# Sliding-window scores as three fp32r products instead of plain fp32, in other banks, with two pieces of other work behind the first quad

## The chip, the cores and the metric

The kernel runs on one core of a Trainium2 chip. The metric is device time in microseconds (us) of one execution. The kernel before the change takes 2162.4 us (median of three runs, 2161.97 to 2162.98).

## What is computed

One step of a one-layer streaming encoder over a prompt of 1024 tokens and a sample of 64, 1024 features wide: retention and sliding-window attention side by side, then cross-attention to 256 memory tokens, then SwiGLU. The change touches the sliding-window attention (SWA): 16 query heads of 64 features share 2 heads of keys and values; a chunk of 64 tokens attends to itself and to the two chunks before it, 192 keys at most.

```python
CHUNK = 64
SWA_HEADS, SWA_KV_HEADS, SWA_HD = 16, 2, 64     # 8 query heads share one head of keys
def swa_attend(q, k, v, bias, sinks, valid):
    s = jnp.einsum('bnqhgd,bnkhd->bnhgqk', q, k, preferred_element_type=jnp.float32) * (SWA_HD ** -0.5)
    s = s + bias.astype(jnp.float32)
    ...
    m = jnp.maximum(jnp.max(s, axis=-1, keepdims=True), sink)
    e = jnp.exp(s - m)
    p = e / (jnp.sum(e, axis=-1, keepdims=True) + jnp.exp(sink - m))
    return jnp.einsum('bnhgqk,bnkhd->bnqhgd', p.astype(v.dtype), v)
```

## The kernel before, in words

All activations lie transposed, features on partitions and tokens on columns. Dense products don't run in plain fp32. `split` (L123 to 125) makes two operands of a tile: ACT copies it, rounded, to the type fp32r (`hi`, L124), and DVE subtracts that from the tile (`lo`, L125). `mm3` (L155 to 159) then adds up three fp32r products, hi x hi, hi x lo and lo x hi, on lines 157, 158 and 159. The large projections do the same in blocks of 128 x 272 columns (L223, L224, L226; recombined in L274), and their last step empties a bank of PSUM in L613 (DVE), scales in L619 (DVE), applies the activation in L621 (ACT) and stores from POOL's queue (L731).

The **SWA phase** (`swa_phase`, about 790 to 955 us of the profiled execution) comes right behind the last of these projections. It has two kinds of work, which are interleaved by hand on PE. The first is attention: 17 chunks of 64 queries (`c`, 0 to 16), in two halves each (`hf`); a chunk and a half are called a *quad* here, since it has four score matrices (two heads of keys `v`, two pairs of heads `i`, each 128 rows by up to 192 keys). The second is *filler*: the dense product of the retention's output with `w_ret_out`, in pieces of half a product, and ahead of it the four pieces (two products, 24 matmuls each) that make the last head's values of the memory.

The loop in `swa` runs i from -2 to 33. In each round PE gets, in this order: `weigh` of quad i-1 (probabilities times values, for a whole chunk), `scores` of quad i+2, `turn` of quad i (transposes of the probabilities), and as many pieces as the generator `fill` hands out. `in_order` makes each of these wait for the last matmul of the one before, so this order is PE's; the order on the other engines comes from a scheduler that keeps the named dependencies.

- `scores`: four plain fp32 matmuls a quad on L1004, the weights being 64 rows of a query tile, the moving operand 64 rows of `kT` with 64 (chunk 0), 128 (chunk 1) or 192 columns. The trace shows each as two instructions, so a quad has eight. Both heads `v` lie on different halves of the rows. The result is the PSUM tile `pss` (tag "s", two banks, one buffer).
- DVE reads each matrix with a fused bias-add and minimum (L1014, four a quad), then L1018. ACT takes four exponentials (L1020) and one for the sinks (L1022). DVE adds and inverts (L1023, L1024), POOL multiplies (L1026, L1031).
- `turn`: values' transposes (L981, copied by ACT on L983), probabilities' transposes (L1043, L1054; copied by ACT on L1047 and DVE on L1056). `weigh`: L1067 into `pout`, copied by DVE on L1071.
- filler: the last products' evacuation is L1229 for `ret` and L1200 for the memory values. Its PSUM tiles `pd` have two buffers, which the values' transposes share.

PSUM pools take banks in the order in which they are opened, so the tag "s" gets the first two, which the last block of the projections before has used. SBUF comes from eight slots per ring ("swin0" to "swin7"), cut by hand: `kT` (keys, 1216 columns), two query tiles of four chunks each, the bias, buffers `lds` for the filler, `vT` and its transposed blocks. Queries come in five loads of four chunks, issued by SP. `begin_swa` issues the phase's first loads while the last projections run; `first_low` (L1153) makes ten `lo` operands of the filler behind the first quad's reads, `later_operands` the others at fixed steps.

Of the kernel before, what the change touches and what calls it, by code (L numbers as in the profile page):

```python
# [11 lines left out]
F32 = mybir.dt.float32  # L12
F32R = mybir.dt.float32r
# [6 lines left out]
P = 128  # L20
# [89 lines left out]
class Kernel:  # L110
# [811 lines left out]
    def swa_phase(self):  # L922
        with ExitStack() as ctx:
            filler = []

            def fill():


                pieces = self.filler()
                yield []  # L930
                yield [pieces] * 6
                count, steps, done = 48 - 10, 2 * 17, 0
                for i in range(steps):
                    goal = count * (i + 1) // steps
                    yield [pieces] * (goal - done)
                    done = goal
                yield [pieces] * 8

            self.store_by = self.nc.gpsimd
            self.swa(ctx, fill())  # L940
            self.store_by = self.nc.sync
# [17 lines left out]
    def swa(self, ctx, fill):  # L959
        nc, tc, io = self.nc, self.tc, self.io  # L960
        if True:
            sw = self.sw = ctx.enter_context(tc.tile_pool(name="sw", bufs=5, reuse_waits="tile"))
            pw = ctx.enter_context(tc.tile_pool(name="pw", bufs=1, reuse_waits="tile", space=PSUM))
            mm = nc.tensor.matmul

            flat, kT, bias, qTs, sinks = self.flat, self.kT, self.bias, self.qTs, self.sinks
            vT = flat[5][:, :KC]
            vts = [flat[4][:, i * P:(i + 1) * P] for i in range(17)] + [flat[0][:, KC + i * P:KC + (i + 1) * P] for i in range(3)]

            def keep():  # L970
                for src, o in ((kT, "o_sk"), (vT, "o_sv")):
                    self.store(io[o][0], src[:, SEQ - P:SEQ])
                    self.store(io[o][1], src[:, SEQ + SMP:KC])

            vtok = {}

# [18 lines left out]

            def scores(c, hf):
                ks, j0, nk = keys(c)
                if hf == 0 and c % 4 == 0 and 0 < c < 13:
                    self.load_queries(qTs, c + 4)
                qT = qTs[c // 4 % 2]  # L1000
                pss = pw.tile([P, 2, 512], F32, tag="s", name="pss")
                for i in range(2):
                    for v in range(2):
                        self.last_mm = mm(pss[:, v, i * NKEY:i * NKEY + nk], qT[rows[v], 2 * hf + i, c % 4, :],  # L1004
                                          kT[rows[v], ks:ks + nk], start=True, stop=True).ins
                quad = lambda x: x.rearrange("p (v h i) -> p v h i", v=2, h=2)[:, :, hf, :]
                snk = quad(sinks)
                t = sw.tile([P, 2, 2, NKEY], F32, tag="t", name="t")
                ps = pss[:, :, :2 * NKEY].rearrange("p v (i n) -> p v i n", n=NKEY)
                bs = bias.rearrange("p (v h i) n -> p v h i n", v=2, h=2)  # L1010
                nm = sw.tile([P, 2, 2], F32, tag="nm", name="nm")
                for v, i in units:
                    u = quad(self.minus)[:, v, i:i + 1]
                    nc.vector.tensor_tensor_reduce(t[:, v, i, :nk], ps[:, v, i, :nk], bs[:, v, hf, i, j0:], -0.125, u,  # L1014
                                                   ALU.add, ALU.min, nm[:, v, i:i + 1])
                den = sw.tile([P, 2, 2], F32, tag="den", name="den")
                es = sw.tile([P, 2, 2], F32, tag="es", name="es")
                ready = nc.vector.tensor_tensor(out=es, in0=snk, in1=nm, op=ALU.add).ins  # L1018
                for v, i in units:
                    nc.scalar.activation(t[:, v, i, :nk], t[:, v, i, :nk], AF.Exp, bias=nm[:, v, i:i + 1], scale=-1.0,  # L1020
                                         accum_out=den[:, v, i:i + 1])
                self.marks.append((ready, nc.scalar.activation(es, es, AF.Exp).ins))  # L1022
                nc.vector.tensor_tensor(out=den, in0=den, in1=es, op=ALU.add)  # L1023
                nc.vector.reciprocal(den, den)  # L1024
                p, n, e = t.rearrange("p v i n -> p (v i) n")[:, :, :min(nk, P)], min(nk, P), None
                nc.gpsimd.tensor_tensor(out=p, in0=p, op=ALU.mult,  # L1026
                                        in1=den.rearrange("p v i -> p (v i)").unsqueeze(2).broadcast_to([P, 4, n]))
                if nk == NKEY:
                    e = sw.tile([P, 2, 2, 64], F32, tag="e", bufs=4, name="e")
                    for v in range(2):  # L1030
                        nc.gpsimd.tensor_tensor(out=e[:, :, v ^ hf, :], in0=t[:, v, :, P:], op=ALU.mult,  # L1031
                                                in1=den[:, v, :].unsqueeze(2).broadcast_to([P, 2, 64]))
                live[c, hf] = t, e

            def turn(c, hf):
                ks, j0, nk = keys(c)
# [23 lines left out]
            def weigh(c, hf):  # L1060
                if hf == 0:
                    return
                parts = live.pop((c, "parts"))
                po = pw.tile([P, 2, 512], F32, tag="out", name="pout")
                for j, part in enumerate(parts):
                    for h, v, val, pT in part:
                        self.last_mm = mm(po[rows[v], h, :256], val[:, rows[v]], pT, start=j == 0, stop=j == len(parts) - 1).ins  # L1067
# [13 lines left out]
            for i in range(-2, n):  # L1081
# [8 lines left out]
                if i == -2:  # L1090
                    with tc.high_priority(), tc.issue_after(self.last_operand):
                        self.tokens(vT, 1, "cvT")
                if i == 2:
                    with tc.issue_after(self.last_operand):
                        self.load_queries(qTs, 4)
                if i == 8:
                    with tc.issue_after(self.last_operand):
                        keep()
# [3 lines left out]

    def begin_swa(self):

        tc, flat = self.tc, [t.rearrange("p a b -> p (a b)") for t in self.ring_tiles(0, KT, "swin", F32)]
        self.flat, self.kT = flat, flat[0][:, :KC]
        self.bias = flat[2][:, :NPAIR * NKEY].rearrange("p (a b) -> p a b", b=NKEY)
        self.qTs = [t[:, :16 * 2 * 64].rearrange("p (i c e) -> p i c e", i=4, c=4) for t in (flat[1], flat[7])]
        self.lds = [t[:, i * 384:(i + 1) * 384] for t in (flat[3], flat[6]) for i in range(5)]
        with tc.high_priority():  # L1110
            self.tokens(self.kT, 0, "ckT")
            self.load_queries(self.qTs, 0)
            for e in range(2):
                src = self.d_rb.rearrange("(p e) c -> e c p", e=2)[e, 63:63 + 64 * 255, :]
                src = src.rearrange("(i c) p -> i p c", c=255)[:, :, :NKEY]
                self.loaded = self.load(self.bias[e * 64:(e + 1) * 64], src)
        self.rets = [self.rings[1].tile(f"ret{k}", slot=i) for k, i in enumerate((0, 1, 4, 5, 6, 7, 2, 3))]
        self.marks = []
        self.first_loads()

    def tokens(self, dst, i, cache):
        self.load(dst[:, :SEQ], self.d_skv[i, :, :SEQ])
# [39 lines left out]
                    self.last_operand = self.load(x, self.d_gate[0][k, :, c0:c0 + n])  # L1162
                self.split(x, self.rets[k][:, 0, c0:c0 + n], self.rets[k][:, 1, c0:c0 + n])

    def load_queries(self, qTs, c):
        nq = min(4, 17 - c)
        src = self.d_sq[:, :, c:c + nq].rearrange("i p c a q -> p i (c a q)")
        self.load(qTs[c // 4 % 2][:, :, :nq, :].rearrange("p i c e -> p i (c e)"), src)

    def ring_tiles(self, i, n, what, dt=F32R):  # L1170
        return [self.rings[i].tile(f"{what}{k}", dt) for k in range(n)]
# [719 lines left out]
```

## Time and profile before

| what | value |
|---|---|
| median of three runs | 2162.4 us (2161.97 to 2162.98) |
| profiled execution, device time | 2165.55 us |
| its span | 2163.7 us |
| mean granted clock of PE | 0.996 |
| plain score matmuls (L1004), instructions | 272, from 790.6 to 951.7 us |

The profile names engines PE (matmul), PEld (its weight loads), DVE, ACT, POOL and SP. A row of a timeline gives start, duration, engine, line, operation, output <- input, tile and element type, and in brackets the idle time of the engine ahead of it with what ended it. Rows on consecutive instructions of one kind are joined (x8). A row of groups gives the count, the sum in us, the mean in ns, and the idle time ahead. fp32r operands are printed as f32 on PE.

### The profile page before, as it was taken

What the parts mean: (1) busy time and instruction counts of PE and PEld (TensorE: products, weight loads), DVE (VectorE), ACT (ScalarE), POOL (GpSimd) and SP (SyncE); (2) the same over time, 40 slices, a digit from 0 to 9 for tenths busy, and PEclk for the clock granted to TensorE, in tenths of its full rate; (3) what the DMA queues carried; (4) which work ended last, traced back from release to release, by engine and by line L of the source; (5) the groups of instructions that cost most, each with busy time, mean ns of one, the idle gap of its engine ahead of it and who ended that gap; (6) DMA issues with size and microseconds to landing.
All of it is one profiled execution on the core that took longest, in us unless ns stands there. A gap on an engine that the chain in (4) does not pass through costs nothing. (4 is left out here: it accounts for less than half of the span.)

```text
span 2163.7 us, 41722 instructions
## 1 busy us (share of the span) xinstructions
PE 2136.0 (99%) x16371; PEld 2084.6 (96%) x16371; DVE 1551.7 (72%) x2912; ACT 874.0 (40%) x1894; POOL 532.4 (25%) x448
## 2 busy tenths in 40 slices
PE   9999999999999999999999999999999999999997
PEld 9999999999999997789999999999999999999997
DVE  8987979786677568656545555678777777777597
ACT  8343434344444356553233333343223222344243
POOL 0000000022353125540000000015556555523531
PEclk9999999999999999999999999999999999999999
DMA  7334454435345485336442121412342232384333
GB/s 263 123 126 123 131 149 129 129 113 159 111 141 190 158 263 173 117 112 211 145 135 92 40 69 61 153 61 101 120 154 88 99 126 92 124 305 153 112 116 112
DMA packets 169893, 290.85 MB, mean 134 GB/s; under 512 B 39266, under 2 KB 96546, under 8 KB 169698
## 3 DMA queue, kind: packets, MB, share of 16 engines
q1 hardware_dynamic: 161666, 269.02, 38.7%
q0 software_dynamic: 3424, 10.82, 1.4%
q10 hardware_dynamic: 4608, 8.36, 1.0%
q8 instruction: 129, 2.11, 0.4%
q14 instruction: 66, 0.54, 0.1%
HBM read 196.97 MB, written 91.16 MB: 133 GB/s over the span
## 5 line engine op out<-in xcount | busy, mean ns | idle before, releaser
L124 ACT CAST wq<-raw 128x512 fp32r<-128x512 f32 (+1 forms) x499 | 302.1, 614 | 564.9 <-PE pq L226 228.8
L125 DVE TENSOR_TENSOR wq<-raw,wq 128x512 fp32r<-128x512 f32 (+1 forms) x499 | 426.8, 860 | 139.0 <-ACT wq L124 136.0
L223 PE MATMUL pq<-T,wq 128*128 128x272 f32 x1832 | 490.6, 287 | 1.7 <-ACT wq L124 0.6
L224 PE MATMUL pq<-T,wq 128*128 128x272 f32 x1832 | 492.0, 288 | 0.0
L224 PE MATMUL pq<-B,wq 128*128 128x272 f32 x1592 | 427.1, 288 | 1.0 <-DVE B L125 1.0
L223 PE MATMUL pq<-B,wq 128*128 128x272 f32 x1592 | 425.4, 287 | 0.1
L226 PE MATMUL pq<-T,wq 128*128 128x272 f32 x1832 | 382.7, 289 | 1.9 <-DVE wq L125 1.9
L201 POOL TENSOR_TENSOR raw<-raw 128x512 f32<-128x512 f32 (+1 forms) x44 | 64.0, 1454 | 1259.0 <-DVE wq L125 531.4
L223 PEld LDWEIGHTS pq<-T,wq 128*128 128x128 f32 x1832 | 344.3, 188 | 3.7 <-issue 1.2
L224 PEld LDWEIGHTS pq<-T,wq 128*128 128x128 f32 x1832 | 343.9, 188 | 0.8 <-issue 0.7
L226 PE MATMUL pq<-B,wq 128*128 128x272 f32 x1592 | 332.0, 289 | 0.0
L224 PEld LDWEIGHTS pq<-B,wq 128*128 128x128 f32 x1592 | 298.8, 188 | 2.4 <-DVE B L125 1.9
L223 PEld LDWEIGHTS pq<-B,wq 128*128 128x128 f32 x1592 | 298.9, 188 | 0.3 <-ACT stage L621 0.3
L226 PEld LDWEIGHTS pq<-T,wq 128*128 128x128 f32 x1832 | 289.6, 189 | 3.6 <-DVE wq L125 2.4
L226 PEld LDWEIGHTS pq<-B,wq 128*128 128x128 f32 x1592 | 251.7, 189 | 0.9 <-issue 0.7
L274 DVE TENSOR_TENSOR u<-pq,u 128x544 f32<-128x544 f32 x177 | 127.1, 719 | 78.5 <-PE pq L226 78.1
L613 DVE TENSOR_TENSOR stage<-pq,u 128x544 f32<-128x544 f32 x112 | 80.1, 717 | 31.0 <-PE pq L226 25.1
L157 PE MATMUL pd<-xc,wq 128*128 128x256 f32 (+1 forms) x256 | 74.5, 291 | 0.0
L159 PE MATMUL pd<-xc,wq 128*128 128x256 f32 (+1 forms) x256 | 74.1, 289 | 0.0
L158 PE MATMUL pd<-xc,wq 128*128 128x256 f32 (+1 forms) x256 | 73.7, 288 | 0.0
L1539 POOL TENSOR_TENSOR stage<-stage,rstd_f 128x544 f32<-128x544 f32 x40 | 63.9, 1606 | 39.1 <-ACT stage L1538 39.1
L204 POOL TENSOR_TENSOR raw<-raw 128x512 f32<-128x512 f32 (+1 forms) x44 | 58.9, 1338 | 52.6 <-DVE wq L125 50.1
(388 smaller groups left out, 4515.3 us busy)
## 6 DMA issues: line engine op xcount, KB each, us to landing
hl<-d_op SPq DMA_DIRECT2D x85, 272.0 KB, 5.3
d_qkv<-stage SPq DMA_DIRECT2D x44, 272.0 KB, 2.3
d_op<-stage SPq DMA_DIRECT2D x44, 272.0 KB, 2.2
d_op<-ht SPq DMA_DIRECT2D x44, 272.0 KB, 3.4
raw<-w_gate SPq DMA_DIRECT2D x22, 512.0 KB, 3.6
raw<-w_up SPq DMA_DIRECT2D x22, 512.0 KB, 5.0
raw<-w_down SPq DMA_DIRECT2D x16, 512.0 KB, 4.9
d_gate<-stage ACTq DMA_DIRECT2D x28, 272.0 KB, 2.9
```

Source lines behind the costliest of these rows:

```text
L124: self.last_cast = self.nc.scalar.copy(hi, src).ins
L125: return self.nc.vector.tensor_tensor(out=lo, in0=src, in1=hi.bitcast(F32), op=ALU.subtract).ins
L157: mm(ps, wh, xh, start=start, stop=False)
L158: mm(ps, wh, xl, start=False, stop=False)
L159: self.last_mm = mm(ps, wl, xh, start=False, stop=stop).ins
L201: tt(out=a11, in0=a11, in1=a21, op=sub)
L223: mm(ps[:, c, :HC], w[:, 0, ks], x[:, 0, cs], start=start, stop=False)
L224: mm(ps[:, c, :HC], w[:, 0, ks], x[:, 1, cs], start=False, stop=False)
L226: self.last_mm = mm(ps[:, c, :HC], w[:, 1, ks], x[:, 0, c * HC:(c + 1) * HC], start=False, stop=stop).ins
L274: add = lambda out, a, b: nc.vector.tensor_tensor(out=out, in0=a, in1=b, op=ALU.add)
L613: nc.vector.tensor_tensor(out=o, in0=ps, in1=sb, op=ALU.add)
L1539: nc.gpsimd.tensor_tensor(out=g, in0=g, in1=r[t], op=ALU.mult)
```

## The change

1. `scores` forms each matrix as three fp32r products, q hi x k hi, q hi x k lo and q lo x k hi. A quad has 12 instructions on PE in place of eight.
2. The keys are split once, 256 columns and then 960, in `begin_swa`. Each half of a chunk's queries (128x256) is split by `split_queries`, the first two in `begin_swa`, the others at the end of `scores`, two halves ahead.
3. Queries are loaded chunk by chunk, 17 loads, into six raw buffers.
4. `pout` gets a pool of its own, opened first, so it takes the two banks that tag "s" had, and "s" the two behind them.
5. `fill` hands out two of the memory values' four pieces between the first and the second quad, and four behind the second, where it handed out none and six.
6. Other slots: `vT` takes over the keys' raw buffer, the bias lies in slot 1 and is loaded earlier, the outputs of the keys (`o_sk`) are stored in `begin_swa`, and `lds` and `vts` are cut anew.

On PE, at the start of the phase, the order changes as follows (`swin_9666` and `swin_9667` are the raw keys and queries, `swin_9668` the `hi` parts, `swin_9669` the `lo` parts of both, `ms` the memory, x2 the two heads `v`):

```order
 L226 MATMUL pq<-T_626,wq 128x272 x2
-L1004 MATMUL pss<-swin_9666,swin_9667 128x64 x8
+L1002 MATMUL pss<-swin_9668 128x64 x2
+L1002 MATMUL pss<-swin_9669,swin_9668 128x64 x2
+L1002 MATMUL pss<-swin_9668,swin_9669 128x64 x2
+L1002 MATMUL pss<-swin_9668 128x64 x2
+L1002 MATMUL pss<-swin_9669,swin_9668 128x64 x2
+L1002 MATMUL pss<-swin_9668,swin_9669 128x64 x2
 L157 MATMUL pd<-wq,ms_7429 128x256
```

The two first quads, which stood together, now stand apart: the second comes 24 products of the values later. On DVE the split of the keys and of the first queries comes in among the last projection's recombinations:

```order
 L274 TENSOR_TENSOR u_9454<-pq,u_9452 128x544
+L125 TENSOR_TENSOR swin_9669<-swin_9666,swin_9668 128x256
+L125 TENSOR_TENSOR swin_9669<-swin_9667,swin_9668 128x256
+L125 TENSOR_TENSOR swin_9669<-swin_9666,swin_9668 128x960
+L125 TENSOR_TENSOR swin_9669<-swin_9667,swin_9668 128x256
 L125 TENSOR_TENSOR wq<-mw,wq 128x512
```

Four subtractions were added there, ahead of a weight's. Behind the first quad's reads DVE has, after the change (`swin_9670` is a buffer of raw queries in the rows of L125 and of the filler in L1222, the memory values' evacuation):

```order
+L1168 TENSOR_TENSOR ret_9686<-swin_9672,ret_9686 128x384
+L1168 TENSOR_TENSOR ret_9687<-swin_9670,ret_9687 128x384
+L1021 TENSOR_TENSOR den<-den,es 128x4
+L125 TENSOR_TENSOR swin_9669<-swin_9670,swin_9668 128x256
+L1222 TENSOR_SCALAR swin_9670<-pd,mtok 128x256
+L125 TENSOR_TENSOR swin_9669<-swin_9670,swin_9668 128x256
+L1012 ISA t,nm<-pss,swin_9667,minus 128x64
```

The evacuation moved ahead of the second quad's reads, with a query's subtraction on either side of it. The diff:

```diff
--- before.py
+++ after.py
@@ -927,8 +927,8 @@
 
 
                 pieces = self.filler()
-                yield []
-                yield [pieces] * 6
+                yield [pieces] * 2
+                yield [pieces] * 4
                 count, steps, done = 48 - 10, 2 * 17, 0
                 for i in range(steps):
                     goal = count * (i + 1) // steps
@@ -960,17 +960,16 @@
         nc, tc, io = self.nc, self.tc, self.io
         if True:
             sw = self.sw = ctx.enter_context(tc.tile_pool(name="sw", bufs=5, reuse_waits="tile"))
+            pout = ctx.enter_context(tc.tile_pool(name="po", bufs=1, reuse_waits="tile", space=PSUM))
             pw = ctx.enter_context(tc.tile_pool(name="pw", bufs=1, reuse_waits="tile", space=PSUM))
             mm = nc.tensor.matmul
 
-            flat, kT, bias, qTs, sinks = self.flat, self.kT, self.bias, self.qTs, self.sinks
-            vT = flat[5][:, :KC]
-            vts = [flat[4][:, i * P:(i + 1) * P] for i in range(17)] + [flat[0][:, KC + i * P:KC + (i + 1) * P] for i in range(3)]
+            flat, bias, sinks = self.flat, self.bias, self.sinks
+            vT = self.kT
+            vts = [flat[s][:, a + i * P:a + (i + 1) * P] for s, a, n in ((5, 0, 17), (4, 1664, 4)) for i in range(n)]
 
             def keep():
-                for src, o in ((kT, "o_sk"), (vT, "o_sv")):
-                    self.store(io[o][0], src[:, SEQ - P:SEQ])
-                    self.store(io[o][1], src[:, SEQ + SMP:KC])
+                self.keep("o_sv")
 
             vtok = {}
 
@@ -995,14 +994,13 @@
 
             def scores(c, hf):
                 ks, j0, nk = keys(c)
-                if hf == 0 and c % 4 == 0 and 0 < c < 13:
-                    self.load_queries(qTs, c + 4)
-                qT = qTs[c // 4 % 2]
                 pss = pw.tile([P, 2, 512], F32, tag="s", name="pss")
+                q, k = [x[(2 * c + hf) % 3] for x in self.qhl], [x[:, ks:ks + nk] for x in self.khl]
                 for i in range(2):
-                    for v in range(2):
-                        self.last_mm = mm(pss[:, v, i * NKEY:i * NKEY + nk], qT[rows[v], 2 * hf + i, c % 4, :],
-                                          kT[rows[v], ks:ks + nk], start=True, stop=True).ins
+                    for a, b in ((0, 0), (0, 1), (1, 0)):
+                        for v in range(2):
+                            self.last_mm = mm(pss[:, v, i * NKEY:i * NKEY + nk], q[a][rows[v], i, :], k[b][rows[v], :],
+                                              start=a + b == 0, stop=a == 1).ins
                 quad = lambda x: x.rearrange("p (v h i) -> p v h i", v=2, h=2)[:, :, hf, :]
                 snk = quad(sinks)
                 t = sw.tile([P, 2, 2, NKEY], F32, tag="t", name="t")
@@ -1031,6 +1029,7 @@
                         nc.gpsimd.tensor_tensor(out=e[:, :, v ^ hf, :], in0=t[:, v, :, P:], op=ALU.mult,
                                                 in1=den[:, v, :].unsqueeze(2).broadcast_to([P, 2, 64]))
                 live[c, hf] = t, e
+                self.split_queries(2 * c + hf + 2)
 
             def turn(c, hf):
                 ks, j0, nk = keys(c)
@@ -1061,7 +1060,7 @@
                 if hf == 0:
                     return
                 parts = live.pop((c, "parts"))
-                po = pw.tile([P, 2, 512], F32, tag="out", name="pout")
+                po = pout.tile([P, 2, 512], F32, tag="out", name="pout")
                 for j, part in enumerate(parts):
                     for h, v, val, pT in part:
                         self.last_mm = mm(po[rows[v], h, :256], val[:, rows[v]], pT, start=j == 0, stop=j == len(parts) - 1).ins
@@ -1090,9 +1089,10 @@
                 if i == -2:
                     with tc.high_priority(), tc.issue_after(self.last_operand):
                         self.tokens(vT, 1, "cvT")
-                if i == 2:
+                if i == -1:
                     with tc.issue_after(self.last_operand):
-                        self.load_queries(qTs, 4)
+                        for c in range(2, 6):
+                            self.load_queries(c)
                 if i == 8:
                     with tc.issue_after(self.last_operand):
                         keep()
@@ -1102,21 +1102,36 @@
 
     def begin_swa(self):
 
-        tc, flat = self.tc, [t.rearrange("p a b -> p (a b)") for t in self.ring_tiles(0, KT, "swin", F32)]
+        tc = self.tc
+        flat = [self.rings[0].tile(f"swin{i}", F32R if i in (2, 3) else F32).rearrange("p a b -> p (a b)") for i in range(KT)]
+        part = lambda *rows: [flat[s][:, a + i * w:a + (i + 1) * w] for s, a, n, w in rows for i in range(n)]
         self.flat, self.kT = flat, flat[0][:, :KC]
-        self.bias = flat[2][:, :NPAIR * NKEY].rearrange("p (a b) -> p a b", b=NKEY)
-        self.qTs = [t[:, :16 * 2 * 64].rearrange("p (i c e) -> p i c e", i=4, c=4) for t in (flat[1], flat[7])]
-        self.lds = [t[:, i * 384:(i + 1) * 384] for t in (flat[3], flat[6]) for i in range(5)]
+        self.khl = [flat[i][:, :KC] for i in (2, 3)]
+        self.qhl = [[t.rearrange("p (i e) -> p i e", i=2) for t in part((i, KC, 3, 256))] for i in (2, 3)]
+        self.qraw = [t.rearrange("p (i e) -> p i e", i=4) for t in part((1, 1536, 1, 512), (4, 0, 1, 512), (7, 0, 4, 512))]
+        self.lds = part((0, KC, 2, 384), (6, 0, 5, 384), (4, 512, 3, 384))
+        self.bias = flat[1][:, :NPAIR * NKEY].rearrange("p (a b) -> p a b", b=NKEY)
+        self.split_done = []
         with tc.high_priority():
             self.tokens(self.kT, 0, "ckT")
-            self.load_queries(self.qTs, 0)
+            self.load_queries(0)
             for e in range(2):
                 src = self.d_rb.rearrange("(p e) c -> e c p", e=2)[e, 63:63 + 64 * 255, :]
                 src = src.rearrange("(i c) p -> i p c", c=255)[:, :, :NKEY]
                 self.loaded = self.load(self.bias[e * 64:(e + 1) * 64], src)
         self.rets = [self.rings[1].tile(f"ret{k}", slot=i) for k, i in enumerate((0, 1, 4, 5, 6, 7, 2, 3))]
+        for a, b in ((0, 256), (256, KC)):
+            self.split(self.kT[:, a:b], self.khl[0][:, a:b], self.khl[1][:, a:b])
+            self.split_queries(a // 256)
+        self.keep("o_sk")
         self.marks = []
         self.first_loads()
+        with tc.issue_after(self.last_operand):
+            self.load_queries(1)
+
+    def keep(self, o):
+        self.nc.gpsimd.dma_start(self.io[o][0], self.kT[:, SEQ - P:SEQ])
+        self.nc.gpsimd.dma_start(self.io[o][1], self.kT[:, SEQ + SMP:KC])
 
     def tokens(self, dst, i, cache):
         self.load(dst[:, :SEQ], self.d_skv[i, :, :SEQ])
@@ -1162,10 +1177,17 @@
                     self.last_operand = self.load(x, self.d_gate[0][k, :, c0:c0 + n])
                 self.split(x, self.rets[k][:, 0, c0:c0 + n], self.rets[k][:, 1, c0:c0 + n])
 
-    def load_queries(self, qTs, c):
-        nq = min(4, 17 - c)
-        src = self.d_sq[:, :, c:c + nq].rearrange("i p c a q -> p i (c a q)")
-        self.load(qTs[c // 4 % 2][:, :, :nq, :].rearrange("p i c e -> p i (c e)"), src)
+    def load_queries(self, c):
+        if c < 17:
+            self.load(self.qraw[c % 6], self.d_sq[:, :, c].rearrange("i p a q -> p i (a q)"))
+
+    def split_queries(self, j):
+        c, hf = divmod(j, 2)
+        if c < 17 and j >= len(self.split_done):
+            self.split_done.append(j)
+            self.split(self.qraw[c % 6][:, 2 * hf:2 * hf + 2, :], self.qhl[0][j % 3], self.qhl[1][j % 3])
+            if hf:
+                self.load_queries(c + 6)
 
     def ring_tiles(self, i, n, what, dt=F32R):
         return [self.rings[i].tile(f"{what}{k}", dt) for k in range(n)]
```

## The prediction

> **What bounds the kernel now.** First the page, for the whole span:
>
> ```profile
> span 2163.7 us, 41722 instructions
> PE 2136.0 (99%) x16371; PEld 2084.6 (96%) x16371; DVE 1551.7 (72%) x2912; ACT 874.0 (40%) x1894; POOL 532.4 (25%) x448
> ```
>
> PE is busy for 2136.0 of 2163.7 us, so a change can gain only what it takes from PE's own work or from PE's few idle microseconds. The phase that changes runs from about 790 to 955 us, so the second view is PE's list of waits between 785 and 1000 us.
>
> ```profile
> PE pss L1004 <- DVE nm L1014: 3.2, 4, 1.4
> PE pss L1004 <- DVE stage L613: 0.8, 1, 0.8
> PE pd L157 <- ACT swin L983: 0.2, 1, 0.2
> ```
>
> Columns: us in total, times, longest. Everything PE waits for here is a bank of scores: once L613 has to empty a bank of the last dense product, four times L1014 has to have read the scores before. The third view is a table of stretches (length, then busy us of each engine, granted clock, DMA share).
>
> ```profile
> core 0: us, PE busy (x) PEld busy (x) DVE busy (x) ACT busy (x) POOL busy (x), PEclk, DMA share, GB/s
> 789.30:793.30 4.00, 2.17 (x21) 1.74 (x19) 3.30 (x13) 3.94 (x10) 0.54 (x1) 0.88 0.80 248
> 792.00:800.00 8.00, 7.70 (x42) 7.59 (x43) 7.21 (x27) 7.54 (x26) 3.24 (x6) 0.57 0.87 274
> 800.00:810.00 10.00, 10.00 (x73) 9.36 (x72) 4.48 (x19) 4.15 (x17) 3.46 (x8) 1.00 0.91 304
> 810.00:820.00 10.00, 8.60 (x63) 6.93 (x60) 8.96 (x33) 7.55 (x27) 3.09 (x3) 1.00 0.70 229
> 820.00:830.00 10.00, 9.36 (x66) 7.36 (x64) 8.76 (x29) 7.80 (x29) 5.11 (x8) 1.00 0.60 189
> 830.00:840.00 10.00, 9.50 (x75) 7.63 (x74) 8.54 (x33) 7.20 (x27) 5.50 (x9) 1.00 0.87 293
> 840.00:955.00 115.00, 115.00 (x876) 92.91 (x877) 78.37 (x336) 70.03 (x273) 64.28 (x101) 1.00 0.33 104
> ```
>
> So the phase has three stages. At the start PE works 2.17 of 4 us, and then runs the next 8 us at a clock of 0.57. From 810 to 840 us DVE is busy for 26.26 of 30 us, PE idles 2.54, and DVE is the bound. From 840 us on PE is busy without a gap, while DVE uses 78 and ACT 70 of 115 us: there only PE's own work counts. The start, in order of time:
>
> ```profile
> 789.39 0.41 PE L226 MATMUL pq<-T,wq 128*128 128x272 f32 x2
> 789.84 0.73 DVE L613 TENSOR_TENSOR stage<-pq,u 128x544 f32<-128x544 f32 x1 [1.50 <-PE pq L226]
> 790.60 0.72 DVE L619 TENSOR_TENSOR stage<-stage,rstd 128x544 f32<-128x544 f32 x1
> 790.62 0.52 PEld L1004 LDWEIGHTS pss<-swin,swin 64*128 64x128 f32 x8 [1.04 <-DVE stage L613]
> 790.62 0.66 PE L1004 MATMUL pss<-swin,swin 64*128 64x64 f32 x8 [0.82 <-DVE stage L613]
> 792.30 1.12 PE L1004 MATMUL pss<-swin,swin 64*128 64x64 f32 x8 [1.01 <-DVE nm L1014]
> 792.52 0.69 DVE L1153 TENSOR_TENSOR wq<-raw,wq 128x512 fp32r<-128x512 f32 x1
> 793.35 0.58 PE L157 MATMUL pd<-wq,ms 128*128 128x256 f32 x1
> 795.37 1.28 ACT L1020 ACT_TABLE_LOAD   x1
> 798.24 0.16 DVE L1023 TENSOR_TENSOR den<-den,es 128x4 f32<-128x4 f32 x1 [0.68 <-ACT es L1022]
> 799.22 0.46 DVE L1200 TENSOR_SCALAR swin<-pd,mtok 128x256 f32<-128x256 f32 x1
> 801.70 0.34 PE L157 MATMUL pd<-ret,wq 128*128 128x384 f32 x1
> ```
>
> PE stands 0.82 us for L613 and 1.01 us for L1014, and the 48 products of values then run slowly, so that the first product with `ret` comes at 801.70.
>
> **The start, with the change.** The scores' tag no longer lies in the banks that L613 empties last, so the first quad can follow the last L226 at 789.8. Two pieces (24 products) stand between it and the second quad, so the reads of L1014 (0.9 us) are done when PE gets there. At full clock a product of 256 columns takes 0.12 us and one of 384 takes 0.18, start to start:
>
> ```profile
> 801.12 0.28 PE L158 MATMUL pd<-wq,ms 128*128 128x256 f32 x1
> 801.24 0.28 PE L159 MATMUL pd<-wq,ms 128*128 128x256 f32 x1
> 804.53 0.34 PE L158 MATMUL pd<-ret,wq 128*128 128x384 f32 x1
> 804.71 0.34 PE L159 MATMUL pd<-ret,wq 128*128 128x384 f32 x1
> ```
>
> PE would be through two small quads (0.5 us each) and 48 x 0.12 = 5.8 us of values at 789.8 + 6.8 = 796.6. It can't go on there: the first `ret` product needs a bank that the values' evacuation (before L1200, now L1222) reads, and the order on DVE puts that behind L613, L619, four reads, the ten subtractions, the sum `den`, and now one query subtraction. In before that row of work reaches `den` at 798.24, held by ACT's table load and exponentials; nothing in the change makes it much shorter. With 0.42 of the new subtraction and 0.46 of the evacuation the bank is free between 798.5 (if `den` comes 0.6 us earlier, its idle time there) and 799.2; I take 798.9. The first `ret` product then comes at 798.9, not at 801.70: **-2.8 us**. What is late next is thus DVE, and PE idles about 2.3 us in one place, where it had idled 1.83 in two.
>
> **The price of a quad on PE.** A quad's length is from its first product to the next group's first:
>
> ```profile
> 806.04 0.71 PE L1004 MATMUL pss<-swin,swin 64*128 64x128 f32 x8
> 806.68 0.33 PE L981 MATMUL pd<-ident,swin 128*128 128x128 f32 x1
> 833.85 0.92 PE L1004 MATMUL pss<-swin,swin 64*128 64x192 f32 x8
> 834.71 0.33 PE L981 MATMUL pd<-ident,swin 128*128 128x128 f32 x1
> ```
>
> That is 0.64 us at 128 columns and 0.86 at 192 (30 of the 34 quads). The eight instructions are four pairs; the two of a pair (v = 0 and 1) use different row halves and run together. So 64 more columns cost a pair 0.22/4 = 0.055 us, 192 cost 0.165, and 0.86 - 4 x 0.165 = 0.20 us is entry and exit. By the rows of 256 and 384 columns above, an fp32r product costs 0.06/128 us a column, which makes 0.09 for 192: half of the plain one. But a pair can't be shorter than its weight loads: in the quad of 64 columns at 790.62 the eight loads take 0.52 us, and with one load at about 0.19 the pitch is 0.33/3 = 0.11 us, though 64 columns would stream in 0.055. No fp32r product under 256 columns stands in this trace, so the pitch of the new pairs is bounded: 0.09 (streaming alone) below, 0.165 (a plain pair's) above. I take 0.11, the load's row, since the shapes of the weights are the same. The quad is then 6 x 0.11 + 0.14 to 0.20 (less than before, if the ends stream only half as long) = 0.80 to 0.86; the middle, 0.83, gives 30 x -0.03 = -0.9 us, and the four small quads, by the same sum 0.1 to 0.25 longer, give back 0.4 to 1.0. In all **0 us** (0.09: 30 x -0.12 = -3.6; 0.165: 6 x 0.165 + 0.2 = 1.19, 30 x 0.33 = +10).
>
> The Trainium skill speaks against this in "TensorE: Matmul & The Clock Gate", Part 3 (row/col tiling): weights load beside running products only where the row groups differ. By it a load (0.11) and a stream (0.09) of one row half would come one after the other, a pitch of 0.20, quads of 1.4 us and +16 us. The trace disagrees: a plain pair would then take 0.11 + 0.165, and the row at 833.85 gives 0.165.
>
> **Splits.** 34 casts on ACT and 34 subtractions on DVE of 128x256 are new, by their nearest rows (cross-attention's operands), above them the row of an operand in this phase, which shares DVE's time with POOL:
>
> ```profile
> L124 ACT CAST co<-cpo 128x256 fp32r<-128x256 f32 x32 | 11.9, 372 | 26.4 <-PE cpo L159 19.2 <-DVE co L125 7.0
> L125 DVE TENSOR_TENSOR co<-cpo,co 128x256 fp32r<-128x256 f32 x32 | 13.5, 422 | 13.3 <-ACT co L124 13.3
> L125 DVE TENSOR_TENSOR ret<-swin,ret 128x320 fp32r<-128x320 f32 x8 | 5.9, 774 | 0.2 <-ACT ret L124 0.2
> ```
>
> Two lie before the first scores. From 840 on 24 x 0.42 = 10 us go into DVE's 37 idle us and 9 into ACT's 45, at two halves' distance from their reader: hidden, and if the cover were gone, up to 10 us. Between 810 and 840 there is no cover: seven halves x 0.42 = 2.9 us (5.4 at 774 ns), while DVE has 3.7 us idle, which are partly waits for PE. I charge +2.0 us (0 to 4). The split of the keys, 256 + 960 columns, is 0.4 + 1.5 us by the same row, in the last dense blocks, where DVE idles:
>
> ```profile
> 783.87 0.72 DVE L274 TENSOR_TENSOR u<-pq,u 128x544 f32<-128x544 f32 x1 [1.60 <-PE pq L226]
> ```
>
> Such an idle stretch takes it, and its first reader comes 6 us later: 0. The queries come in 17 loads, not 5; four of these stand between operands' loads on SP's queue behind the stage stores of POOL, which issue at 792 to 796. Their readers come after 803; a late one would hold ACT's cast, the operands' casts behind it, and the fillers. Bias and `o_sk` go earlier, off PE's path: 0.
>
> **Sum.** -2.8 + 0 + 2.0 = -0.8 us against the profiled execution's 2165.55 (span 2163.7). That execution is 3.15 us above the median of 2162.4; the difference is taken over: 2161.6.
>
> **Rivals.**
> - *Plain price* (slower). If fp32r below 256 columns streams as slowly as a whole plain product, a pair takes 2 x 0.165 = 0.33, the quad 2.2 us, 30 x 1.3 = +39: 2201. For it: no such form runs in this trace; against it: 256 to 384 columns cost by the column. It decides from a pitch of about 0.14 on, where 30 x 6 x 0.03 exceeds the start's gain. A milder form, a pitch of 0.165, gives +9: 2171.
> - *Halves one after the other*: twelve loads of 0.11 and no pairs, 1.5 us, +21: 2183. Against it: plain pairs run together.
> - *The clock drops again.* Before 792 PE idled 1.83 of 4 us and the clock fell to 0.57 for 8 us, 3.4 us lost; the stall at 818 (1.4 us, the longest of the list) left it at 1.00. My 2.3 us before 798.9 is above both, in one piece. Then -2.8 + 3.4, and less waiting after it: about +1.5, 2164. The Trainium skill, same page, Part 1, gives half rate after an idle window of about 3.4 us; by that 2.3 us would leave the clock alone, but the row at 789.30 fell with less.
> - *Stalls vanish as well* (faster): DVE gets its work spread by the earlier start, +2.0 becomes -1 and the clock holds: -4 to -6, 2157.
> - *DVE and ACT late throughout*, the splits at 774 ns: +4, 2166.
>
> **How the numbers follow.** What this measurement can tell from no change is 0.2%, 4.3 us. Chances: forecast 0.42, clock again 0.20, stalls vanish 0.10, late splits 0.08, pitch 0.165 0.08, plain price 0.07, halves in turn 0.04, the skill's rule 0.01 (2178). The range leaves out the last three and a tail of the fastest, and takes in the pitch's bounds: 2156 to 2172. The first three cases but for a small part, and most of the late splits, are within 0.2%; half of the vanishing stalls, and a pitch of 0.09 in the forecast (0.05), are faster: 0.10 in all. Slower: 0.08 + 0.07 + 0.04 + 0.01 + 0.05 of late work = 0.25. Same: 0.65.
>
> **What would show it.** Quads of 0.80 to 0.86 us at L1002 (1.2, 1.5 or 2.2 by the rivals); no wait for L613; a granted clock of 1.00 up to 797, and what it is behind the wait for L1222; the first `ret` product near 798.9; waits of L1002 for L1012 between 806 and 840 grown from 2.2 to some 4 us; no idle PE after 845. It is wrong if a quad's length is off by over 0.1 us, or if queries arrive late.

## The result and the profile after

The changed kernel takes 2173.7 us (median of six runs, 2167.76 to 2176.36) against 2163.17 us (six runs, 2161.97 to 2165.84) before: a ratio of 1.0045, 95% interval 1.0035 to 1.0056, 0.45% slower (the two medians alone give 1.0049). The forecast was 2161.6, its range ended at 2172. The profiled execution took 2172.69 us with a span of 2170.9. One execution of an experiment below, that with the stores from another queue, took 2967.39 us at a mean clock of 0.653, and is left out of its figures.

PE's list of waits, 785 to 1000 us, in the changed kernel:

```profile
PE pp L1042 <- POOL t L1024: 4.6, 2, 3.0
PE pss L1002 <- DVE nm L1012: 4.2, 3, 2.4
PE pd L157 <- DVE swin L1222: 1.4, 1, 1.4
PE pp L1053 <- POOL e L1029: 0.8, 2, 0.5
```

The first row and the last are new: transposes of the probabilities (L1042, L1053) wait for POOL's multiplications by 1/den. Nothing of the kind was in the list before. The stretches of the changed kernel, and under them the one between 806 and 840 us of before, which the prediction had in pieces:

```profile
789.30:793.30 4.00, 4.00 (x39) 3.82 (x39) 3.93 (x15) 3.97 (x10) 1.62 (x3) 1.00 1.00 353
806.00:840.00 34.00, 29.63 (x229) 25.10 (x228) 29.23 (x103) 25.27 (x89) 15.16 (x20) 0.95 0.73 235
840.00:955.00 115.00, 109.66 (x893) 91.05 (x893) 81.53 (x328) 71.04 (x271) 59.53 (x94) 0.97 0.32 100
```

```profile
806.00:840.00 34.00, 31.46 (x229) 25.50 (x229) 28.64 (x106) 25.50 (x94) 14.25 (x21) 1.00 0.74 242
```

The start is busy and at full clock. But from 840 us on, where PE had been busy for 115.00 of 115 us, it is busy for 109.66, and the granted clock is 0.97. That is 5.34 us of waiting, and two drops of the clock, which lose 1.7 us each (their rows stand in the last section): 3.4 us, or 0.03 of the 115.

Four points in time give the sums: PE's first possible product of scores (the end of the last L226), then the third, the eleventh and the last quad. In the changed kernel:

```profile
787.91 0.41 PE L226 MATMUL pq<-T,wq 128*128 128x272 f32 x2
...
801.68 0.33 PE L1002 MATMUL pss<-swin 64*128 64x128 f32 x2
...
842.53 0.36 PE L1002 MATMUL pss<-swin 64*128 64x192 f32 x2
...
959.52 0.36 PE L1002 MATMUL pss<-swin 64*128 64x192 f32 x2
```

The two rows of before that the prediction doesn't have:

```profile
842.98 0.92 PE L1004 MATMUL pss<-swin,swin 64*128 64x192 f32 x8
...
951.10 0.92 PE L1004 MATMUL pss<-swin,swin 64*128 64x192 f32 x8
```

| stretch | before | after | difference |
|---|---|---|---|
| L226's end (789.80; 788.32) to the third quad | 16.24 | 13.36 | -2.9 |
| third to eleventh quad | 36.94 | 40.85 | +3.9 |
| eleventh to last quad | 108.12 | 116.99 | +8.9 |
| sum | 161.30 | 171.20 | +9.9 |

The sum agrees with the difference of the medians, 10.5 us. (The two profiled executions differ by 7.14 only: the changed one came to this phase 1.5 us earlier, and took 1.3 us less behind the last quad. The bad-order run below, whose code ahead of these quads and behind them is that of before, was 2.5 us earlier and 1.7 us quicker there, so this is scatter.)

Where do the 8.9 us arise? PE's longest wait is at 911.49, and POOL's rows around it tell why. Before:

```profile
900.32 1.29 POOL L1026 TENSOR_TENSOR t<-t,den 128x512 f32<-128x512 f32 x1
901.57 0.75 POOL L1031 TENSOR_TENSOR e<-t,den 128x128 f32<-128x128 f32 x2
902.27 0.81 POOL L121 DMA_DIRECT2D d_swa<-osb  x1
906.23 0.76 POOL L121 DMA_DIRECT2D d_swa<-osb  x1 [3.14 <-DVE nm L1014]
907.01 1.05 POOL L1026 TENSOR_TENSOR t<-t,den 128x512 f32<-128x512 f32 x1
```

After, with DVE's inversion of that quad's `den` and PE's transposes:

```profile
903.35 0.58 POOL L121 DMA_DIRECT2D d_mix<-swin  x1 [1.39 <-DVE swin L1251]
904.43 0.17 DVE L1022 RECIPROCAL den<-den 128x4 f32<-128x4 f32 x1
904.94 0.77 POOL L121 DMA_DIRECT2D d_swa<-osb  x1 [1.00 <-DVE den L1022]
909.61 0.76 POOL L121 DMA_DIRECT2D d_swa<-osb  x1 [3.89 <-DVE nm L1012]
910.38 1.05 POOL L1024 TENSOR_TENSOR t<-t,den 128x512 f32<-128x512 f32 x1
911.49 0.66 PE L1042 MATMUL pp<-ident,t 128*128 128x128 f32 x4 [3.04 <-POOL t L1024]
```

The pair of stores of the attention's output (`d_swa`, two DMAs issued by POOL) keeps POOL for 4.7 us before, 5.4 after, from the first issue to the end of the second. The DVE instruction in the brackets is unlikely to be the reason: at another pair of before, the same gap (2.85 us, ahead of 867.73) is put down to "issue", which is time in which the engine waited for nothing that the profile shows. Before, the multiplication of quad 21 ran ahead of the pair. After, it stands behind it: its `den` is there at 904.6 (L1022's end), yet POOL begins it at 910.38, and PE stands. The order of the two programs shows the swap at two places (here for quad 21; `t` is the multiplication, quad 9 reads alike):

```
 before                                   after
 L121 DMA d_mix<-swin 128x320             L121 DMA d_mix<-swin 128x320
 L1026 TENSOR_TENSOR t<-t,den             L121 DMA d_swa<-osb 128x4x128 x2
 L1031 TENSOR_TENSOR e<-t,den x2          L1024 TENSOR_TENSOR t<-t,den
 L121 DMA d_swa<-osb 128x4x128 x2         L1029 TENSOR_TENSOR e<-t,den x2
```

Two swaps, and two waits for `t` in the list. The theory to test, A: POOL's order makes the loss. The rivals: B, the splits' work on DVE and ACT makes the quads late, whatever POOL's order; C, the loads or the start's edits do.

### The profile page after: what moved, and what is told of

It reads as the page before. It is cut to its first block, busy times and chain, and to the rows that moved or that the text cites. A ratio compares the mean times of both kernels' runs of the same rounds, so it can differ in the third digit from the quotient of the medians.

```text
span 2170.9 us, 42114 instructions
## 1 busy us (share of the span) xinstructions
PE 2137.1 (98%) x16507; PEld 2089.5 (96%) x16507; DVE 1567.7 (72%) x2948; ACT 887.5 (41%) x1930; POOL 531.9 (25%) x448
## 4 chain that ended last, share of the span: by engine, by line
PE 85%; DVE 6%; DMA 4%; issue 2%; ACT 1%; POOL 1%; SPq 0%; POOLq 0%; DVEq 0%; ACTq 0%
PE pq L226 17%; PE pq L224 17%; PE pq L223 17%; PE pd L157 8%; PE pd L159 8%; PE pd L158 8%; DVE wq L125 2%; PE pout L1066 1%; PE pss L1002 1%; DVE T L125 1%; PE pk L766 1%; DMA hl<-d_op 1%; PE pp L1042 1%; DMA swin<-d_sq 1%; PE po L159 1%
## 5 line engine op out<-in xcount | busy, mean ns | idle before, releaser
L125 DVE TENSOR_TENSOR wq<-raw,wq 128x512 fp32r<-128x512 f32 (+1 forms) x499 | 426.5, 859 | 137.8 <-ACT wq L124 134.9
L226 PE MATMUL pq<-T,wq 128*128 128x272 f32 x1832 | 382.7, 289 | 1.9 <-DVE wq L125 1.9
L226 PE MATMUL pq<-B,wq 128*128 128x272 f32 x1592 | 332.0, 289 | 0.0
L226 PEld LDWEIGHTS pq<-T,wq 128*128 128x128 f32 x1832 | 289.6, 189 | 3.6 <-DVE wq L125 2.4
L226 PEld LDWEIGHTS pq<-B,wq 128*128 128x128 f32 x1592 | 251.7, 189 | 0.9 <-issue 0.7
L1561 POOL TENSOR_TENSOR stage<-stage,rstd_f 128x544 f32<-128x544 f32 x40 | 64.0, 1609 | 39.1 <-ACT stage L1560 39.1
```

The lines of the kernel that those rows point to most:

```text
L125: return self.nc.vector.tensor_tensor(out=lo, in0=src, in1=hi.bitcast(F32), op=ALU.subtract).ins
L226: self.last_mm = mm(ps[:, c, :HC], w[:, 1, ks], x[:, 0, c * HC:(c + 1) * HC], start=False, stop=stop).ins
L1561: nc.gpsimd.tensor_tensor(out=g, in0=g, in1=r[t], op=ALU.mult)
```

## The experiments

Each was timed beside the kernel before, in five rounds; ratios are against it.

**The stores behind the multiplications.** POOL's order is put back in the changed kernel:

```diff
-                nc.gpsimd.tensor_tensor(out=p, ...)
+                scaled = nc.gpsimd.tensor_tensor(out=p, ...)
...
+                self.last_scaled = scaled.ins
...
-                    for m in range(0, KT, 4):
-                        self.store(self.d_swa[...], ...)
+                    with tc.issue_after(self.last_scaled):
+                        for m in range(0, KT, 4):
+                            self.store(self.d_swa[...], ...)
```

> The changed kernel, with one thing added: the stores of the attention's output on POOL's queue must come behind the multiplications by 1/den that were emitted before them, so no pair of stores stands ahead of a quad's multiplication. Theory A (order on POOL): the two waits of PE's transposes for POOL's t (4.6 us, with 0.8 for e) go, and with them the two drops of the granted clock they bring after 840 us (2 x 1.7 us): 2173.7 - 8.7 = about 2165. Theory B (the splits' own work on DVE and ACT makes the quads late, whatever POOL's order): no change, 2172 to 2175. Theory C (the queries' loads or the start): no change.

Measured: 2164.56 us (12 runs), 1.0007 (0.9997 to 1.0017): 9.1 us of the loss are gone, with every split still in place. Its waits from 785 to 1000 us, and its last stretch:

```profile
PE pss L1002 <- DVE nm L1012: 3.1, 2, 2.0
PE pd L157 <- DVE swin L1224: 2.2, 1, 2.2
PE pd L157 <- ACT swin L982: 0.5, 1, 0.5
```

```profile
840.00:955.00 115.00, 115.00 (x970) 95.43 (x970) 87.72 (x359) 77.39 (x293) 63.88 (x101) 1.00 0.34 105
```

No wait for POOL, and PE is busy for 115.00 us again at a clock of 1.00, beside more work on DVE (87.72) than in either kernel. B and C fall: the splits and the loads are all still there.

**The stores from another queue.** In the changed kernel, `self.store(self.d_swa...)` becomes a DMA on SP's queue, where loads are issued too.

```diff
-                        self.store(self.d_swa[m:m + 4, :, c0:c0 + n].rearrange("m p c -> p m c"),
+                        self.load(self.d_swa[m:m + 4, :, c0:c0 + n].rearrange("m p c -> p m c"),
```

> The changed kernel, with the stores of the attention's output issued by SP and not by POOL. Theory A: POOL is free of the pair that held it for 4.7 to 5.4 us, so both waits for POOL's t go: about 2165, or a little less. Theory B and C: no change, 2172 to 2175. A wait of SP's queue for the output would show as late operand loads.

Measured: 2162.81 us (11 runs), 0.9996 (0.9988 to 1.0005), and PE doesn't wait at all between 840 and 955 us. The second, independent way to take the pair out of the multiplication's way removes the loss as well.

**Plain products, no splits, all else of the change.**

```diff
-                q, k = [x[(2 * c + hf) % 3] for x in self.qhl], [x[:, ks:ks + nk] for x in self.khl]
+                q, k = self.qraw[c % 6][:, 2 * hf:2 * hf + 2, :], self.kT[:, ks:ks + nk]
...
-                self.split_queries(2 * c + hf + 2)
+                if hf:
+                    self.load_queries(c + 6)
```

> The changed kernel with plain fp32 products in the scores, from the raw queries and keys, and without any split; banks, pieces, loads by chunk and the earlier bias stay (the values get a buffer of their own). Theories A and B: the splits are gone, and POOL's order is the old one, so the start's gain of about 2.8 us stands alone: 2160 (2158 to 2162). Theory C: loads or start cost, and it stays above 2166.

Measured: 2162.59 us (12 runs), 0.9997 (0.9989 to 1.0006). The order on POOL is that of before, and the loss is gone, so the loads by chunk are not its cause. It is 2.6 us above the expectation. The edit takes away the three products together with the splits, so it doesn't tell which of the two the scheduler answers to.

**Banks and pieces alone**, in the kernel before:

```diff
-                yield []
-                yield [pieces] * 6
+                yield [pieces] * 2
+                yield [pieces] * 4
...
+            pout = ctx.enter_context(tc.tile_pool(name="po", bufs=1, reuse_waits="tile", space=PSUM))
             pw = ctx.enter_context(tc.tile_pool(name="pw", bufs=1, reuse_waits="tile", space=PSUM))
...
-                po = pw.tile([P, 2, 512], F32, tag="out", name="pout")
+                po = pout.tile([P, 2, 512], F32, tag="out", name="pout")
```

> The kernel before with the two other edits alone: the output's banks first, and two pieces of values between the first and the second quad. Theories A and B: no split, old order on POOL, -2.8 us at the start: 2160 (2158 to 2162), and no drop of the clock near 792. If the idle time at the start drops the clock all the same, 2163.

Measured: 2161.67 us (11 runs), 0.9991 (0.9982 to 0.9999): 1.5 us faster by the medians, less than the 2.8 us expected. The sign is that of the start's gain; its size isn't settled by an interval that is 3.7 us wide. In its trace the start, from the end of L226 to the third quad, takes 13.1 us, against 16.24 before, and the clock holds.

**The bad order alone, in the kernel before.** The reverse test: nothing of the change is in it but POOL's two swaps. The multiplications of quads 9 and 21 are held back and emitted behind the next pair of stores.

```diff
+                if 2 * c + hf in (9, 21):
+                    held.append(scale)
+                else:
+                    scale()
...
+                    with tc.issue_after(last):
+                        while held:
+                            held.pop()()
```

> The kernel before, with plain products and no split, and with the multiplications of the quads 9 and 21 moved behind the pair of stores that stood behind them: the order that POOL has in the changed kernel, and nothing else of the change. Theory A (order on POOL): two waits of PE for POOL's t, 1.5 to 3 us each, and a drop of the clock behind one or both of them (1.7 us each): 2163.2 + 5 to 9 = 2168 to 2172. Theory B (the splits' work on DVE and ACT has to be there for the loss): less than 2 us, 2163 to 2165.

Measured: 2173.79 us (6 runs), 1.0043 (1.0026 to 1.0059): the time of the changed kernel, without a split, a load or a bank of it. It is somewhat above A's range, and its profiled execution was the fastest of the six. That one shows the waits, and under them its last stretch:

```profile
PE pp L1048 <- POOL t L1027: 5.4, 2, 2.8
```

```profile
840.00:955.00 115.00, 109.49 (x818) 88.27 (x818) 70.81 (x309) 64.12 (x250) 58.30 (x93) 0.99 0.31 100
```

DVE and ACT have no instruction more than in the kernel before, and are busy for less of these 115 us (there 78.37 and 70.03), so their load has no part in it. In this execution the two waits and one drop of the clock (0.99) make 7.7 us from the eleventh to the last quad; that the slower ones lose the clock a second time is likely, but not shown.

**Splits without the start's edits**: the changed kernel with `[]` and six pieces, and `pout` in the common pool.

```diff
-                yield [pieces] * 2
-                yield [pieces] * 4
+                yield []
+                yield [pieces] * 6
...
-                po = pout.tile([P, 2, 512], F32, tag="out", name="pout")
+                po = pw.tile([P, 2, 512], F32, tag="out", name="pout")
```

> The changed kernel with the start undone: scores in the first two banks again, and none and six pieces in place of two and four. POOL's order is that of the changed kernel. If the start's edits are worth 2.8 us with the splits as well, 2173.7 + 2.8 = 2176 to 2177, with waits for L613 and for the second quad's bank. If the time after 840 us had come from the start's edits, 2165 to 2168.

Measured: 2176.57 us (6 runs), 1.0059 (1.0043 to 1.0074). It has the two swaps and two waits for POOL's `t`, 4.8 us together. By the medians the start's edits are worth 2.9 us beside the splits too, though the intervals of the two kernels overlap; in the traces the start takes 17.0 us without them and 13.36 with them.

**Banks, pieces, and the stores on SP**: both edits shown above, in the kernel before.

> The kernel before with the banks and the pieces, and with the stores of the attention's output issued by SP. After 840 us PE did not wait, so nothing is to be had there; between 806 and 840 one pair of stores stands on POOL. 2161 to 2162, as without it; 2160 if that pair counts.

Measured: 2162.46 us (12 runs), 0.9995 (0.9986 to 1.0005): moving the stores gains nothing where no multiplication that PE waits for stands behind them.

**The evacuation earlier**, with banks and pieces, in the kernel before. The first product of values is evacuated between the fifth and the sixth of the ten subtractions of `first_low`, and the first quad's `den` comes behind them:

```diff
-            self.first_low()
+            self.first_low(self.first[:5], self.marks[0][0])
...
+                if t == 0:
+                    with tc.issue_after(self.first_low(self.first[5:], self.values_out)):
+                        self.first_scale()
```

> The kernel before with the banks and the pieces, and on DVE with the first product of values evacuated in the middle of the ten subtractions, and the first quad's den behind them. The wait of the first product with ret for that evacuation (1.5 us in the banks-and-pieces run) goes: 2161.7 - 1.5 = about 2160. If the last subtractions are what the product then waits for, no change: 2161.7.

Measured: 2160.59 us (12 runs), 0.9987 (0.9977 to 0.9998), the fastest of all, and the wait of the `ret` product for the evacuation is no longer in the list. It beats both kernels: 2.8 us less than before by the ratio, 0.4 to 5.0 by its interval.

**All traces side by side.** From the eleventh quad's first product to the last quad's is the part of the phase in which the changed kernel loses its 8.9 us, and scatter elsewhere in the execution has no part in it. In the seven programs without the swaps (before, the stores behind the multiplications, the stores from another queue, plain products, banks and pieces, the same with the stores on SP, the evacuation earlier) it takes 108.1 us. In the three with them it takes 115.3 (splits without the start's edits), 115.8 (the bad order alone) and 117.0 (the changed kernel).

## Why the prediction was wrong, step by step

- **The start** held: -2.8 us forecast, -2.9 measured, by the way that was named. The first quad runs right behind L226, the clock stays at 1.00 here, and what is late next is L1222's evacuation:

```profile
796.32 0.15 DVE L1021 TENSOR_TENSOR den<-den,es 128x4 f32<-128x4 f32 x1
796.72 0.48 DVE L1222 TENSOR_SCALAR swin<-pd,mtok 128x256 f32<-128x256 f32 x1
797.35 0.41 PE L157 MATMUL pd<-ret,wq 128*128 128x384 f32 x1 [1.38 <-DVE swin L1222]
```

From the end of L226 that is 9.0 us, where 9.1 was forecast. The idle time was 1.4, not 2.3 us, and the rival of a second drop of the clock did not come true here. In the run with the stores behind the multiplications the wait was 2.2 us, and the clock did drop behind it (0.51 from 799.0 to 802.5 us). That the size came out to 0.1 us is in part luck: before, the clock stood at 0.50 for 6.83 us of the profiled execution (792.31 to 799.14), but for 3.41 us only in that of the bad-order run, whose start is the same code. There the start took 14.6 us, not 16.24, and the gain against it would be 1.3 us.

- **The price of a quad** held: pairs at 0.11 us. The time from the first product to the next group's is 0.85 us, against 0.86 before, so the plain price, the halves in turn and the rule of the Trainium skill ("TensorE: Matmul & The Clock Gate", Part 3) are all out. (For a pitch of 0.165 the prediction gives +10 in one place and +9 in another; its sum is 9.9.)

```profile
815.72 0.36 PE L1002 MATMUL pss<-swin 64*128 64x192 f32 x2 [2.38 <-DVE nm L1012]
815.92 0.38 PE L1002 MATMUL pss<-swin,swin 64*128 64x192 f32 x4
816.14 0.27 PE L1002 MATMUL pss<-swin 64*128 64x192 f32 x2
816.25 0.38 PE L1002 MATMUL pss<-swin,swin 64*128 64x192 f32 x4
816.57 0.70 PE L1042 MATMUL pp<-ident,t 128*128 128x128 f32 x4
```

- **The splits between 806 and 840 us**: +2.0 forecast, +3.9 measured. The instructions are about what was charged for ACT, and on DVE 30% dearer in the mean (the median is 423 ns, the longest takes 1.79 us); over 800 to 962 us:

```profile
L125 DVE TENSOR_TENSOR swin<-swin,swin 128x256 fp32r<-128x256 f32 x29 | 15.9, 550 | 0.0
...
L124 ACT CAST swin<-swin 128x256 fp32r<-128x256 f32 x29 | 11.7, 405 | 35.2 <-PE pss L1002 29.2 <-ACT es L1020 3.1 <-issue 2.8
```

PE is busy for 1.83 us less of these 34 than before, which is about the forecast term; 1.7 us are the clock (0.05 x 34), which dropped behind the wait of 2.38 us at 815.72, and 0.4 us are not accounted for. That a stall of this length can also cost clock was priced at the start alone. It doesn't always: where the clock held, in the two runs with splits and without the swaps, third to eleventh quad took 38.9 and 39.1 us, which is the +2.0 of the forecast against 36.94. But its reason is right in part only: the run with plain products, without any split, took 38.1, with banks and pieces alone it was 36.9. So some 1.2 of the 2.0 us come with the loads by chunk, the earlier bias or the new slots, which the prediction put at 0. Which of them it is was not tried.

- **The step that failed** is "hidden" for the splits from 840 us on, 0 us in the sum where 8.9 were measured; of the signs that the prediction named, "no idle PE after 845" is the one that failed. DVE and ACT did have the room, as the runs with POOL's order put back show (115.00 us busy). But the sum looked only at whether the work fits, and it took the order of the other engines as it was. With the splits, the scheduler placed two pairs of `d_swa` stores ahead of a multiplication on POOL, an engine that is busy for a quarter of the span and that stood in no list of waits. POOL's queue was never compared between the two programs, though their order alone shows both swaps. The price of a swap is read from before: a pair holds POOL 4.7 us, and the prediction never set that against the time by which a quad's `t` comes early. The runs show it from both sides: with the order put back, 9.1 us go; with the order alone, 10.1 us come (2173.79 against 2163.73 beside it). All programs here with the splits and the stores free on POOL's queue have the swaps (the changed kernel and the one without the start's edits); of those without splits only the one into which they were put by hand has them. So they come with the splits or with the three products that need them, which no run here parts. By which of its estimates the scheduler came to it is open.

- **What the range missed** is then one mechanism, waiting and clock together: 5.34 and 3.4 us after 840. Of the slower rivals, most were prices of PE, which the pitch of 0.11 us refutes; the others were the clock at the start and late splits on DVE and ACT. None was about another engine's queue.

## What to carry to other kernels

An edit that adds work to engines with room can still reorder an engine that it doesn't touch, when a scheduler sets the order: compare the order on every engine, the idle ones first, and look for what moved ahead of an instruction that the bound engine needs. A DMA issued from POOL's queue is to be counted with the time for which it holds POOL (here 4.7 to 5.4 us for a pair), not with the duration of its rows (0.8 us each). A wait on a PE that was always busy is to be priced with the clock that it may lose, too.

## What the runs showed of the hardware

In this phase the granted clock fell to 0.50 for 3.41 us at a time (at the start of before once for 6.83), which loses 1.7 us. In the changed kernel, the last row being a drop by itself:

```profile
911.50:916.50 5.00, 4.74 (x20) 4.25 (x22) 1.00 (x3) 2.44 (x10) 2.58 (x5) 0.66 0.05 16
849.00:856.00 7.00, 5.24 (x24) 4.56 (x26) 4.62 (x14) 2.67 (x11) 6.55 (x11) 0.76 0.42 138
816.00:822.00 6.00, 6.00 (x38) 5.13 (x38) 3.58 (x18) 6.00 (x23) 2.07 (x4) 0.72 0.84 253
912.62:916.04 3.42, 3.42 (x13) 3.42 (x12) 0.76 (x2) 2.01 (x10) 1.46 (x3) 0.50 0.00 0
```

0.34 x 5.00, 0.24 x 7.00 and 0.28 x 6.00 are each 1.7 us. Ahead of the first three PE had waited 3.04, 1.51 and 0.52 (at 850.24 and 851.41), and 2.38 us; the wait of 1.38 us at 797.35 left the clock at 1.00. The Trainium skill ("TensorE: Matmul & The Clock Gate", Part 1) gives half rate after an idle window of about 3.4 us. The length of the drops agrees with that window; but here less idle time than a whole window was enough, and the length of a wait alone doesn't decide. In the bad-order run the clock held through a wait of 2.77 us (the first two rows), and with the stores from SP through one of 2.08 us ahead of 814.77 (the third), while in the run without the start's edits it fell behind one of 1.87 us ahead of 818.70.

```profile
908.38 0.66 PE L1048 MATMUL pp<-ident,t 128*128 128x128 f32 x4 [2.77 <-POOL t L1027]
902.00:913.00 11.00, 8.18 (x61) 6.40 (x58) 4.88 (x25) 5.15 (x21) 5.44 (x9) 1.00 0.36 114
812.00:820.00 8.00, 5.92 (x52) 4.71 (x51) 7.06 (x30) 7.16 (x28) 2.56 (x6) 1.00 0.60 177
```

The times of the drops suggest why. In the changed kernel they begin at 817.05, 851.18 and 912.62, which are 34.13 and 61.44 us apart, 10 and 18 times 3.413. If the clock is set anew at the end of each such step, the idle time within one step counts. In the steps that end at these three drops PE was idle for 2.08, 1.80 and 2.54 of 3.41 us; the wait of 2.77 us that left the clock alone falls into two steps of its run, 1.71 us in the one and 1.06 in the other. In all ten traces each step of this phase with 1.80 us idle or more brought a drop, and none with 1.71 or less did, save one (1.24 us, at the start of the bad-order run, where two quads of 64 columns stand in the step). This is read from the traces, and no run was made to try it; by it, it is in part luck whether a wait of 2 or 3 us costs 1.7 us more. Such drops are likely a part of the scatter, too: of the changed kernel's six runs the fastest (2167.76) has a mean clock of 0.998, the slowest (2176.36) one of 0.995.

The pair of stores holds POOL by more than its two rows of 0.8 us: between them lie 3.14 us in the rows of before and 3.89 in those of after. And a split's subtraction, 0.42 us alone, took 1.79 us beside a multiplication on POOL:

```profile
909.96 1.79 DVE L125 TENSOR_TENSOR swin<-swin,swin 128x256 fp32r<-128x256 f32 x1
```

The Trainium skill ("SBUF — State Buffer", Who interferes with whom) says that a DVE instruction with two inputs in SBUF contends with a POOL instruction that reads SBUF; this row and POOL's at 910.38 agree. Which of DVE's instructions lengthen the hold of a pair was not tried.
